# A hybrid decoder layer on one core: a rotary group, three weight splits, two modulation turns and a weave of products change their places

## The chip, the core and the metric

The kernel runs on one core of one Trainium2 chip. The metric is the device time of one launch in microseconds. The kernel before takes 1086.85 us as the median of three runs (1086.14 to 1087.83).

A core has TensorE (PE, matmuls; its weight loads are listed as PEld), VectorE (DVE), ScalarE (ACT), GpSimd (POOL) and SyncE (SP, which here only issues DMAs). Each engine works through its own instructions in a fixed order and waits on semaphores for the others.

## The reference

The layer has two sub-layers on 1024 tokens of width 1024, all in float32. Cut to what matters here:

```python
mod = silu(c) @ w_ada + b_ada
sh1, sc1, g1, sh2, sc2, g2 = split(mod, 6)
h = rmsnorm(x, pre_w_mix) * (1 + sc1) + sh1
aq, ak, av, hq, hf, hi, hg = split(h @ w_in)
aq, ak = partial_rope(aq), partial_rope(ak)      # 16 of each head's 64 dims turn
attn = rmsnorm(sliding_window_sink_attention(aq, ak, av, sinks), attn_out_w)
rec = rmsnorm(hgrn2_chunkwise(silu(hq), 1 - f, hi, log(f)), hg_norm_w) * silu(hg)
x = x + g1 * rmsnorm(concat(attn, rec) @ w_out, post_w_mix)
h = rmsnorm(x, pre_w_mlp) * (1 + sc2) + sh2
x = x + g2 * rmsnorm(square(relu(h @ w_up)) @ w_down, post_w_mlp)
```

Attention has 8 query heads of 64 on 2 key/value heads and a window of 128 tokens, so a block of 128 queries looks at its own block of keys and at the one before.

## The kernel before

**Exact products from rounded parts.** TensorE multiplies numbers in a rounded 32-bit format. Each operand is therefore split: ScalarE copies it into a high half (`hi`, with the names ending in `h`), and VectorE subtracts that from the original to get the low half (`lo`, ending in `l`). A product is three matmuls: high with high, high with low, low with high. `load_split` splits a loaded weight.

**First projection (loop at lines 469 to 523, about 22 to 58 us).** For the first half of the tokens, a loop over the eight 128-wide slices `kb` of the model width turns the normalised x (`first_T`), applies scale and shift while it evicts the result from PSUM (`first_evac`, which makes `hhi` and `hlo`), and multiplies with six weight units: 0 to 3 are queries, 4 is keys, 5 is values (`first_mm`). The scale `a1` and shift `sh1` (with its negative `ns1`) of slices 4, 5 and of 6, 7 come from the conditioning vector: `mod_sum` adds up eight blocks of w_ada on VectorE into `macc`, and `mod_turn` turns the sum on TensorE into `pmt`, reduces it on VectorE and computes `a1`, `sh1` and `ns1`. `mod_turn` is called in the steps kb = 3 and kb = 5, between the units 0 to 3 and the units 4 and 5. In this stage the order on all compute engines is pinned to the order in the program (`pin`).

**The second half of the tokens and attention (lines 700 to 901, about 58 to 188 us; the generator is `attention`, from line 621).** Keys and values of the second half are projected at once; its four query units come later (`q_later`), as pieces of one matmul each in a list, `feed_q`. `feed(us)` takes pieces from that list until the given time is used up at 0.227 us a piece; so it fills TensorE while the softmax of the attention blocks runs on other engines. `weave` mixes the pieces of two units: cuts [6, 9, 12, ...] give six pieces of the one, six of the other, then three of each in turn. Each unit has 24 pieces and needs one of two PSUM banks (`mm_ps`) from its first piece until ScalarE has evicted it behind its last. Behind the queries, `values` puts the value products of the recurrent heads into the same list. Their weights `whv0` to `whv7` are split by `split_hv`.

Attention runs over eight blocks of 128 tokens, as generators that stop between stages, which `step(tb)` moves on:

- stages 1 and 2: scores `sc` on TensorE, mask copy into `comb` on VectorE; maximum `mx`, `nm`, `sd`; eight exponentials with their sums on ScalarE; `den`, `rd` and the scaling of `comb`, half on VectorE and half on GpSimd
- stage 3: `comb` is turned into `pT`; VectorE cuts it into `pc` (own block) and `pp` (block before); `spread` multiplies the block before by its norm (`rb`)
- stage 4: `oT`, the output; its square `sqa`, `aT`, and the sum of squares `sqr`
- stages 5 and 6: `sqr` is turned into `ssp` and summed to `ssc`; GpSimd computes the root; `dg` and the product `rb` spread it

**Rotary.** A query or key tile has its turning rows gathered by DMA (`gather`, three DMAs a tile), multiplied by tables and added (`rotate`, three VectorE instructions on 96 or 64 rows), and scattered back by DMA (`scatter`). For the second half of the tokens there are two groups: group 0 holds two query units and the keys, group 1 the other two query units. Both are done by `rope_late` and `scatter_late`, at the end of block 0's round.

**What sets the order.** In this stage the order of TensorE is pinned, that of SyncE until the end of block 0's round. VectorE, ScalarE and GpSimd are not pinned; the compiler orders them. A few steps are told to follow a marked instruction: `rope_late`, `split_hv` and `mod_sums` take a mark ("sqr", "rb", "omlb", "dg"), which is the latest instruction recorded under that name, and all VectorE instructions of that call are placed somewhere behind it. `mod_sums(n)` moves the sums for the gate g1 and for the second sub-layer on by n blocks of w_ada; the list holds 27 such moves, nine to a sum, and what is left of them runs behind the last block.

After attention come the recurrent heads (products `phf`, `phq`, `phg`), the output projection and the MLP.

Of the kernel before, what the change touches and what calls it, by code (L numbers as in the profile page):

```python
# [13 lines left out]
ALU = mybir.AluOpType  # L14
AX = mybir.AxisListType

P = 128
D = 1024
KB = D // P
# [28 lines left out]
def hybrid_layer(ctx: ExitStack, tc: tile.TileContext, I, out, dbg=None):  # L48
    nc = tc.nc
    ACT, DVE, POOL, PE, SP = (Queue(tc, e) for e in (nc.scalar, nc.vector, nc.gpsimd, nc.tensor, nc.sync))  # L50
# [281 lines left out]
    def mod_turn(q, mk):  # L332
        pst = mk(f"pmt{q[0]}")
        for j in range(4):
            PE.transpose(pst[:, j * P:(j + 1) * P], macc1[q][:, j * P:(j + 1) * P], ident)
        red = small.tile([P, 4], F32, tag="mred", name=f"mred1_{q[0]}")
        DVE.tensor_reduce(red, pst.rearrange("p (j k) -> p j k", j=4), AX.X, ALU.add)
        c = slice(2 * q[0], 2 * q[0] + 2)
        s2 = small.tile([P, 2], F32, tag="m1s", name=f"m1s{q[0]}")
        DVE.tensor_tensor(s2, red[:, 2:4], bT[:, 8 + c.start:8 + c.stop], ALU.add)  # L340
        DVE.tensor_tensor(sh1[:, c], red[:, 0:2], bT[:, c], ALU.add)
        DVE.scalar_tensor_tensor(a1[:, c], s2, 1.0, prew1s[:, c], ALU.add, ALU.mult)
        DVE.tensor_scalar(ns1[:, c], sh1[:, c], -1.0, None, ALU.mult)
# [67 lines left out]
    def first_mm(kb, us, part, ts=slice(0, 512)):  # L411
        bh, bl = (h[:, ts] for h in hh[kb][0])
        for u in us:
            pst, (ah, al) = pu[u][:, ts], unit(u, kb)
            if part == 0:
                PE.matmul(pst, lhsT=ah, rhs=bh, start=(kb == 0 and ts.start == 0), stop=False)
                PE.matmul(pst, lhsT=al, rhs=bh, start=False, stop=False)
            else:
                PE.matmul(pst, lhsT=ah, rhs=bl, start=False, stop=(kb == KB - 1))
# [49 lines left out]
    for kb in range(1, KB):  # L469
        q = nextq.get(kb)  # L470
        if kb == 3:
            mod_sum((2, 0), (7,))
        if kb == 7:
            rbx = tp_ps("rbx")
            PE.matmul(rbx, lhsT=ones, rhs=dgx.rearrange("p a t -> p (a t)"), start=True, stop=True)
        first_evac(0, kb, xT0[kb])
        if kb + 1 < KB:
            first_wq(kb + 1)
        else:
            for j in range(3):  # L480
                DVE.tensor_tensor(xT1[j], xT1[j], rbx, ALU.mult)
            first_evac(1, 0, xT1[0])
            first_evac(1, 1, xT1[1])
        if kb == 3:
            norm_scale(0, 1, ACT)
            pin(True, SP)
            for hf in range(2):
                for tb in range(4, TB):
                    load_x(tb, (hf,))
            pin(False, SP)  # L490
        first_mm(kb, range(4), 0)
        if q:
            mod_mm(q)
            mod_copy(q)
        if kb in (3, 5):
            mod_turn((kb // 2 + 1, 0), tp_ps if kb == 3 else a_ps)
        first_mm(kb, (4, 5), 0)
        if kb + 1 < KB:
            first_wql(kb + 1)
        if q:  # L500
            mod_fold(q)
        if kb in (1, 3, 5):
            first_kv((kb + 1) // 2, DVE)
        if kb < 5:
            mod_sum(*{1: ((2, 0), (0, 4, 1)), 2: ((2, 0), (5, 2, 6, 3)),
                      3: ((3, 0), (0, 4, 1)), 4: ((3, 0), (5, 2, 6, 3, 7))}[kb])
        if kb + 1 < KB:
            xT0.append(first_T(0, kb + 1, a_ps if kb in (2, 3, 6) else tp_ps))
        for tb, hf in {4: ((4, 0), (5, 0)), 5: ((6, 0), (7, 0), (4, 1), (5, 1)), 6: ((6, 1), (7, 1))}.get(kb, ()):
            norm_sq(tb, (hf,))  # L510
        if kb in (5, 6):
            for j in range(4 * kb - 20, 4 * kb - 16):
                xT1.append(load_raw(hT_ if j < 6 else m_, f"xT1_{j}", I["xT1"][j]))
        if kb == 6:
            hgw = cload("hgw", [P, 1], pool=tiny1)
            lbt = cload("lbt", [P, 2, 4], pool=tiny1)
            cosT, sinT = ([load_raw(hv_, f"rope{i}_{th}", I["rope"][i, th]) for th in range(2)] for i in range(2))
        if kb == 6:
            norm_rstd(1, 0, 4)
            dgx = t_("dgx", (P, 4, P))  # L520
            DVE.tensor_tensor(dgx, ident.unsqueeze(1).broadcast_to([P, 4, P]),
                              rx[1].unsqueeze(2).broadcast_to([P, 4, P]), ALU.mult)
        first_mm(kb, range(6), 1)
# [17 lines left out]
    marks = {}  # L541

    def feed(us):
        while us > 0 and feed_q:
            fn, w = feed_q.pop(0)
            fn()
            us -= w
# [60 lines left out]
    fle = cload("fle", [P, P], pool=XA)  # L608
# [12 lines left out]
    def attention(tb):  # L621
# [43 lines left out]
        pc = w_(f"pc{tb}", (P, 2, 4, P))  # L665
        pp = w_(f"pp{tb}", (P, 2, 4, P)) if tb else None
        for mp in range(2):
            pT = tp_ps(f"pT{tb}_{mp}")
            for j in range(4):
                PE.transpose(pT[:, j * P:(j + 1) * P], c[:, 4 * mp + j, :], ident)  # L670
            pT3 = pT.rearrange("p (h q) -> p h q", h=4)
            DVE.tensor_tensor(pc[:, mp], pT3, fle.unsqueeze(1).broadcast_to([P, 4, P]), ALU.mult)
            if tb:
                marks["pp"] = DVE.tensor_tensor(pp[:, mp], pT3, pc[:, mp], ALU.subtract).ins
        spread(tb - 1)
        if 3 <= tb <= 5:
            mod_sums(1, "rb")
        yield
        o_ps = tp_ps(f"oT{tb}")
# [13 lines left out]
        sqr = small.tile([P, P], F32, tag="sqr", bufs=1, name=f"sqr{tb}")  # L693
# [10 lines left out]
        rb = pa.tile([P, 512], F32, tag="aps", name=f"rb{tb}")  # L704
# [17 lines left out]
    for kb in range(KB):  # L722
# [4 lines left out]
        if kb < 6:  # L727
            u = (0, 1, 4, 2, 3, 5)[kb]
            t = evac(0, u, pu[u])
# [44 lines left out]
    def rope_late(mark, i):  # L774
        old, DVE.last = DVE.last, marks[mark]
        rotate(r1[2 * i], r1[2 * i + 1], 64 if i else 96, 1)
        DVE.last = old

    def scatter_late(i):
        for j, t in enumerate(qs[1][2:] if i else qs[1][:2] + [ks[1]]):  # L780
            scatter(t, r1[2 * i], j)

    def q_later(u):
        pst = bank(f"pq1_{u}")

        def done():
            gather(evac(1, u, pst()), *r1[2 * (u // 2):2 * (u // 2) + 2], u % 2)

        queue3(pst, [unit(u, kb) for kb in range(KB)], hhalf(1), 0.227, done)
# [11 lines left out]
    def weave(calls, cuts):  # L801
        a = len(feed_q)
        lists = []
        for call in calls:
            call()
            lists.append(feed_q[a:])
            del feed_q[a:]
        for lo, hi in zip([0] + cuts, cuts + [3 * KB]):
            for fns in lists:
                feed_q.extend(fns[lo:hi])  # L810
# [13 lines left out]
        mods += [modcols(3, half, m_, sh2), modcols(4, half, m_, sc2)]  # L824
    for u in range(2):
        q_later(u)
    weave([lambda: q_later(2), lambda: q_later(3)], [6, 9, 12, 15, 18, 21])

    def step(tb):
        if tb < TB:  # L830
            next(att[tb], None)
# [10 lines left out]
    def split_hv(ks, mark):  # L842
        old, DVE.last = DVE.last, marks[mark]
        for kb in ks:
            if kb < 3:
                wv = w_(f"whv{kb}", (P, 2, 512), F32R)
                parts = {"h": wv[:, 0], "l": wv[:, 1]}
                whv.append(load_split(lambda name, dt: parts[name[-1]], f"whv{kb}", None, raw=hvr[kb]))
            else:
                whv.append(load_split(g_, f"whv{kb}", None, raw=hvr[kb]))  # L850
            if kb < 3:
                load_hv(kb + 5)
        DVE.last = old
# [11 lines left out]
    step(1)  # L865
    feed(2.0)
    step(0)
    feed(2.6)
    for t in range(TB):
        step(t)  # L870
        if t == 0:
            split_hv(range(3, 5), "sqr")
            values_all()
        if t == 1:
            split_hv(range(5, 7), "sqr")
        if t == 1:
            mod_sums(1)
        if 1 < t < 6:
            mod_sums(1, "sqr")
        feed(3.3 if t == 0 else 2.2 if t < 6 else 2.8 if t < 7 else 99)  # L880
        step(t + 2)
        if t == TB - 1:
            pin(False, PE)
        step(t)
        step(t + 2)
        feed(1.0 if t < 6 else 1.8)
        if t > 5:
            mod_sums(1, "dg")
        step(t)
        if t == TB - 1:  # L890
            spread(t)
        step(t + 1)
        if t == 0:
            for i in range(2):
                rope_late("rb", i)
                scatter_late(i)
            pin(False, SP)
        if t == 1:
            split_hv(range(7, KB), "rb")
        feed(4.2 if t == 0 else 2.6 if t < 7 else 99)  # L900
    mod_sums(len(sums), "rb")
    gactx.close()
    Z = x1ctx.enter_context(tc.tile_pool(name="poolZ", bufs=1))
# [886 lines left out]
    for step, (_, t, k) in enumerate(order):  # L1790
# [13 lines left out]
        if k >= 3 and t < 3:  # L1804
            tb = t + 4 * th
# [150 lines left out]
```

## Time and profile before

| | |
|---|---|
| median of three runs | 1086.85 us |
| the profiled execution | 1085.65 us |
| its span | 1083.9 us |
| mean granted TensorE clock | 0.996 of full speed |
| VectorE busy | 803.5 us |
| ScalarE busy | 584.9 us |
| GpSimd busy | 357.3 us |

The page gives busy times over the span of one profiled execution, and the timeline lists instructions by their start (us from the start of the span), duration, engine, operation and tiles; in square brackets stands how long the engine was idle before and what ended that. Nearly all instructions have one line, that of the helper that issues them (line 39), so they are told apart by their tiles. Matmuls overlap: one of 512 columns lasts 0.39 us and the next starts 0.22 to 0.23 us behind it. A list of waits gives total microseconds, number and the longest. A table of stretches gives each engine's busy time in the stretch, the granted TensorE clock as a share of full speed, the share of the DMA engines and GB/s.

### The profile page before, as it was taken

How to read it: one execution, taken by the hardware profiler on the slowest of the kernel's cores; microseconds unless marked ns; L12 is line 12 of the kernel's file. 1: busy time of each engine (PE TensorE's matmuls, PEld its weight loads, DVE VectorE, ACT ScalarE, POOL GpSimd, SP SyncE). 2: the span in 40 equal slices, each digit the busy share in tenths (PEclk: the TensorE clock that was granted, in tenths of full speed). 3: DMA queues.
4: the chain of work that ended last, by engine and by line, in shares of the span. 5: the costliest groups of instructions: out<-in, count | busy, mean ns of one | idle time of the engine just before them, and what ended most of it. 6: DMA issues, size and time to landing. Idle time of an engine off the chain costs nothing.

```text
span 1083.9 us, 15842 instructions
## 1 busy us (share of the span) xinstructions
PE 1065.2 (98%) x5339; PEld 865.4 (80%) x5339; DVE 803.5 (74%) x1317; ACT 584.9 (54%) x1205; POOL 357.3 (33%) x449
## 2 busy tenths in 40 slices
PE   8999999999999999999999999999999999999996
PEld 6787666888888888888888888888888888888885
DVE  4876787888766664558877767677777886899786
ACT  4555354446456655576655555555665544455434
POOL 1221111233325653423434344444333434300014
PEclk9999999999999999999999999999999999999998
DMA  9930301644211252323676777767998888997537
GB/s 355 367 117 28 120 1 34 202 146 140 75 59 56 90 177 95 128 89 129 210 257 231 248 244 232 270 222 250 298 378 308 276 291 279 330 307 250 174 96 138
DMA packets 104865, 208.60 MB, mean 192 GB/s; under 512 B 13840, under 2 KB 14352, under 8 KB 104784
## 3 DMA queue, kind: packets, MB, share of 16 engines
q1 hardware_dynamic: 89296, 160.03, 43.0%
q0 software_dynamic: 15200, 47.20, 14.4%
q8 instruction: 42, 0.69, 0.3%
q10 hardware_dynamic: 288, 0.36, 0.1%
q14 instruction: 39, 0.32, 0.1%
HBM read 150.52 MB, written 55.05 MB: 190 GB/s over the span
## 4 chain that ended last, share of the span: by engine, by line
PE 88%; DVE 5%; DMA 4%; ACT 1%; SPq 1%; issue 1%; POOL 0%; DVEq 0%; ACTq 0%; POOLq 0%
PE pda L39 16%; PE pua L39 14%; PE pdc L39 8%; PE po L39 8%; PE puc L39 7%; PE pu L39 4%; PE phg L39 4%; PE phq L39 4%; PE pdb L39 4%; PE phf L39 4%; PE pub L39 4%; PE pv L39 3%; DMA wa<-wada 2%; PE pq L39 2%; PE o L39 1%; PE oT L39 1%
## 5 line engine op out<-in xcount | busy, mean ns | idle before, releaser
L39 POOL TENSOR_TENSOR b<-b,b 128x512 f32<-128x512 f32 x64 | 88.6, 1384 | 214.5 <-DMA b<-w_dn 214.1
L39 ACT ACTIVATE dw<-dwr 128x512 fp32r<-128x512 f32 x72 | 45.4, 630 | 51.4 <-DMA dwr<-td 29.9
L39 ACT ACTIVATE s<-s 128x512 f32<-128x512 f32 x84 | 53.0, 631 | 33.4 <-DVE s L39 32.0
L39 DVE TENSOR_TENSOR acc<-pda,acc 128x512 f32<-128x512 f32 x68 | 46.7, 687 | 18.3 <-PE pda L39 17.7
L39 DVE TENSOR_TENSOR dw<-dwr,dw 128x512 fp32r<-128x512 f32 x72 | 54.5, 758 | 6.9 <-ACT dw L39 6.9
L39 POOL TENSOR_TENSOR rrf<-ssf,mhalf 128x1 f32<-128x1 f32 x7 | 7.7, 1105 | 106.2 <-DVE ssf L39 106.2
L39 POOL DMA_DIRECT2D td<-b x64 | 36.3, 566 | 19.0 <-POOL b L39 19.0
L39 DVE TENSOR_TENSOR wt<-s,wt 128x512 fp32r<-128x512 f32 x42 | 37.1, 883 | 2.4 <-ACT wt L39 2.1
L39 ACT ACTIVATE s<-pua 128x512 f32<-128x512 f32 x28 | 16.7, 597 | 37.3 <-PE pua L39 34.6
L39 ACT ACT_TABLE_LOAD x28 | 35.9, 1283 | 1.7 <-PEq L1949 1.2
L39 POOL DMA_DIRECT2D b<-w_dn x64 | 34.4, 540 | 2.7 <-issue 2.7
L39 DVE SCALAR_TENSOR_TENSOR macc<-wada,cs,macc 128x512 f32<-128x512 f32 x42 | 33.2, 790 | 2.4 <-DMA wada<-wada 1.7
L39 ACT ACTIVATE comb<-comb,nm 128x128 f32<-128x128 f32 x64 | 24.8, 389 | 18.0 <-DVE nm L39 14.0
L39 DVE TENSOR_TENSOR wt<-a,wt 128x512 fp32r<-128x512 f32 x42 | 33.8, 805 | 0.9 <-ACT wt L39 0.9
L39 POOL TENSOR_TENSOR comb<-comb,rd 128x512 f32<-128x512 f32 x8 | 11.8, 1469 | 66.6 <-DVE rd L39 31.2
L39 PE MATMUL pua<-bt_0h,wt 128*128 128x512 f32 x84 | 32.7, 389 | 0.0
L39 PE MATMUL pua<-bt_1h,wt 128*128 128x512 f32 x84 | 32.7, 389 | 0.0
L39 PE MATMUL pua<-bt_2h,wt 128*128 128x512 f32 x84 | 32.7, 389 | 0.0
L39 PE MATMUL pua<-bt_3h,wt 128*128 128x512 f32 x84 | 32.7, 389 | 0.0
L39 ACT ACTIVATE wt<-s 128x512 fp32r<-128x512 f32 x42 | 26.3, 627 | 10.2 <-DVE s L39 10.0
L39 DVE TENSOR_TENSOR acc<-pdc,acc 128x512 f32<-128x512 f32 x36 | 24.7, 685 | 6.9 <-PE pdc L39 6.5
L39 DVE TENSOR_TENSOR s<-puc,s 128x512 f32<-128x512 f32 x14 | 9.7, 691 | 26.9 <-issue 25.5
(794 smaller groups left out, 3698.2 us busy)
## 6 DMA issues: line engine op xcount, KB each, us to landing
dur<-ud SPq DMA_DIRECT2D x112, 256.0 KB, 4.3
wada<-wada SPq DMA_DIRECT2D x64, 256.0 KB, 3.5
b<-w_dn POOLq DMA_DIRECT2D x64, 256.0 KB, 5.0
td<-b POOLq DMA_DIRECT2D x64, 256.0 KB, 3.4
dwr<-td SPq DMA_DIRECT2D x64, 256.0 KB, 4.0
a<-w_u SPq DMA_DIRECT2D x56, 256.0 KB, 4.5
dwr<-w_dn SPq DMA_DIRECT2D x48, 256.0 KB, 4.6
ud<-s SPq DMA_DIRECT2D x42, 256.0 KB, 3.4
```

Source lines behind the costliest of these rows:

```text
L39: ins = op(*args, **kw)
```

## The change

- In the first projection, kb = 3 now multiplies unit 4, then turns the modulation, then multiplies unit 5; kb = 5 multiplies units 4 and 5 and then turns.
- Query units 2 and 3 are woven 15 pieces and 15, then three of each in turn, in place of six and six.
- Rotary group 0 of the second half follows a new mark, block 0's last `pc`, and its scatters are issued there; group 1 stays at the end of block 0's round.
- Value weights 5, 6 and 7 are split behind block 1's `sqr`; before, 5 and 6 were, and 7 behind the multiply by `rb` at the end of block 1's round.
- In block 0's round the second feed grows from 1.0 to 1.5 us and the third shrinks from 4.2 to 3.8.
- One more move of the modulation sums runs in attention, at block 2.

```diff
-        if kb in (3, 5):
-            mod_turn((kb // 2 + 1, 0), tp_ps if kb == 3 else a_ps)
-        first_mm(kb, (4, 5), 0)
+        if kb == 3:
+            first_mm(kb, (4,), 0)
+            mod_turn((2, 0), tp_ps)
+            first_mm(kb, (5,), 0)
+        else:
+            first_mm(kb, (4, 5), 0)
+        if kb == 5:
+            mod_turn((3, 0), a_ps)
...
-            DVE.tensor_tensor(pc[:, mp], pT3, fle.unsqueeze(1).broadcast_to([P, 4, P]), ALU.mult)
+            marks["pc"] = DVE.tensor_tensor(pc[:, mp], pT3, fle.unsqueeze(1).broadcast_to([P, 4, P]), ALU.mult).ins
...
-        if 3 <= tb <= 5:
+        if 2 <= tb <= 5:
             mod_sums(1, "rb")
...
-    weave([lambda: q_later(2), lambda: q_later(3)], [6, 9, 12, 15, 18, 21])
+    weave([lambda: q_later(2), lambda: q_later(3)], [15, 18, 21])
...
     step(0)
+    rope_late("pc", 0)
+    scatter_late(0)
     feed(2.6)
     for t in range(TB):
         step(t)
...
         if t == 1:
-            split_hv(range(5, 7), "sqr")
+            split_hv(range(5, KB), "sqr")
...
-        feed(1.0 if t < 6 else 1.8)
+        feed(1.5 if t == 0 else 1.0 if t < 6 else 1.8)
...
         if t == 0:
-            for i in range(2):
-                rope_late("rb", i)
-                scatter_late(i)
+            rope_late("rb", 1)
+            scatter_late(1)
             pin(False, SP)
-        if t == 1:
-            split_hv(range(7, KB), "rb")
-        feed(4.2 if t == 0 else 2.6 if t < 7 else 99)
+        feed(3.8 if t == 0 else 2.6 if t < 7 else 99)
```

## The prediction

> **What bounds the kernel now.** I read the page first, then the waits of TensorE over the whole program, then the timeline around the longest two, then the granted clock in short stretches.
>
> ```profile
> span 1083.9 us, 15842 instructions
> PE 1065.2 (98%) x5339; PEld 865.4 (80%) x5339; DVE 803.5 (74%) x1317; ACT 584.9 (54%) x1205; POOL 357.3 (33%) x449
> ```
>
> TensorE is busy for 98% of the span, so what can be won without removing matmuls is in its gaps and in stretches at a lower clock. The list of its waits (total us, times, longest) is short:
>
> ```profile
> PE pv L39 <- DVE whv7l L39: 2.3, 1, 2.3
> PE pq L39 <- ACT qT L39: 2.3, 1, 2.3
> PE pmt L39 <- DVE macc L39: 0.8, 1, 0.8
> PE rb L39 <- DVE dg L39: 0.5, 1, 0.5
> PE oT L39 <- DVE pp L39: 0.4, 1, 0.4
> ```
>
> The first three and the last lie beside code that the diff touches. The first gap, in order of time:
>
> ```profile
> 83.25 0.39 PE L39 MATMUL pq<-hlo,wq1h 128*128 128x512 f32 x1
> 83.47 0.39 PE L39 MATMUL pq<-hhi,wq1l 128*128 128x512 f32 x1
> 85.54 0.57 ACT L39 ACTIVATE qT<-pq 128x512 f32<-128x512 f32 x1
> 86.17 0.50 PE L39 MATMUL pq<-hhi,wq0h 128*128 128x512 f32 x1 [2.31 <-ACT qT L39]
> 90.53 0.39 PE L39 MATMUL pq<-hhi,wq2h 128*128 128x512 f32 x1
> ```
>
> Late query products are fed in pieces; a stream of them starts one every 0.22 to 0.23 us (83.25, 83.47). Counting feeds (9, 14, 14, 18, 9, 12 pieces), the row at 86.17 is piece 55: the first of the fourth query unit, woven in after six pieces of the third. It needs the PSUM bank of the second unit, whose eviction sits on ScalarE behind the exponentials of block 0 and ends at 86.11. The row at 90.53 is piece 64.
>
> The second gap, and the same place one block later:
>
> ```profile
> 119.80 0.39 PE L39 MATMUL pv<-whv7h,hhi 128*128 128x512 f32 x1
> 121.77 0.69 DVE L39 TENSOR_TENSOR whv7l<-whv7r,whv7h 128x512 fp32r<-128x512 f32 x1
> 122.52 0.79 PE L39 MATMUL pv<-whv7l,hhi 128*128 128x512 f32 x1 [2.33 <-DVE whv7l L39]
> 126.87 0.50 PE L39 MATMUL pv<-whv7l,hhi 128*128 128x512 f32 x1
> 136.24 0.39 PE L39 MATMUL pv<-whv7l,hhi 128*128 128x512 f32 x1
> 139.00 0.50 PE L39 MATMUL pv<-whv,hhi 128*128 128x512 f32 x1
> ```
>
> A value product waits for the low half of the last value weight, which VectorE splits only behind block 1's multiply by rb. Behind the gap the work is slow too. In the stretches (busy us of PE, PEld, DVE, ACT, POOL; then the clock granted):
>
> ```profile
> 83.00:87.00 4.00, 1.70 (x11) 0.96 (x11) 1.06 (x3) 3.12 (x15) 0.75 (x1) 1.00 0.00 1
> 122.00:126.00 4.00, 3.48 (x9) 1.52 (x11) 1.52 (x4) 1.91 (x9) 1.45 (x1) 0.57 0.51 177
> 126.00:130.00 4.00, 4.00 (x26) 2.49 (x24) 2.06 (x3) 1.20 (x2) 0.00 (x0) 1.00 0.41 151
> 105.00:125.00 20.00, 17.38 (x96) 11.55 (x96) 18.22 (x38) 10.13 (x42) 3.72 (x4) 0.94 0.40 121
> ```
>
> Around the first gap the clock stays at 1.00; from the end of the second gap it is 0.57 over four microseconds, then 1.00 again. VectorE is busy 18.2 of 20 us around there: it is the engine that could be late next.
>
> **The change part by part.** The profiled execution took 1085.65 us with a span of 1083.9; the median of the three runs shown is 1086.85, that is 1.2 us above the profiled one. I make the sum against the profiled time and add the 1.2 at the end.
>
> *Weave of the third and fourth query unit (15, 18, 21).* The order changes, the 48 pieces don't. Piece 55 becomes one of the third unit, whose bank is free, and would start at 83.47 + 0.23 = 83.70 where it starts at 86.17: 2.5 us won. The fourth unit's first piece is now number 64, at 90.53 - 2.5 = 88.0, and its bank is free at 86.11: that wait is gone, with 1.9 us to spare. Gain 2.5 us (bounds 0, if the wait only moves, and 2.5).
>
> *First late rotary group behind block 0's pc.* It issues three VectorE instructions of 96 rows and three scatter transfers on SyncE's in-order queue.
>
> ```profile
> 86.14 1.77 SPq L39 DMA_DIRECT2D r<-qT  x3
> DMA to landing us min/median/max: 2.7/3.1/3.5
> 91.90 1.29 DVE L39 TENSOR_TENSOR pc<-pT,c_fle 128x512 f32<-128x512 f32 x2 [0.29 <-PE pT L39]
> 94.91 0.17 DVE L39 TENSOR_TENSOR den<-sm,es 128x8 f32<-128x8 f32 x1 [1.72 <-ACT comb L39]
> 107.22 1.88 DVE L39 TENSOR_TENSOR r<-r,rope 96x512 f32<-96x512 f32 x3
> ```
>
> Three such operations take 1.88 us (the row at 107.22). Behind pc VectorE idles 1.72 us until block 1's exponentials are summed, so the group fits into a hole and at most 0.2 us of it shows. Its gathers are issued from 86.14 to 87.91 (first row), which no part of the change moves, since the eviction that they follow ends at 86.11; the last is issued at about 87.3 and landed by 90.8 at the latest of the second row. pc ends at 93.19 now; the chain in front of it (copies of the scores, maximum) can start 1.4 to 1.7 us earlier, so it will end at about 91.5: 0.7 us behind the landing. In SyncE's queue the three scatters stand ahead of the gathers of units three and four, which follow evictions that start at 102.31 now: no cost. Only the scores of block 4 use the scattered rows, three blocks later. Cost 0 (bounds 0 and 0.6: if the three run behind block 1's softmax sums, block 0's aT and sqr are that much late).
>
> *Feeds of block 0 (1.5 and 3.8 in place of 1.0 and 4.2): 7 and 17 pieces for 5 and 19.* The count stays; two value pieces now follow the last query piece at once, and need the third unit's bank.
>
> ```profile
> 102.31 1.30 ACT L39 ACTIVATE qT<-pq 128x512 f32<-128x512 f32 x2
> 102.57 0.40 PE L39 MATMUL pq<-hhi,wq7l 128*128 128x512 f32 x1
> ```
>
> The first of these evictions ends at about 102.9, where the value piece would be due at 102.57 + 0.23 = 102.80; with the row-to-row delay of 0.06 seen at 86.11 to 86.17 that is a new wait of 0.2 us (bounds 0 and 0.4).
>
> *Three weight splits behind block 1's sqr.* The product that stalled is due at 119.80 + 0.23 = 120.03 and ran at 122.52: 2.49 us. From that product to the first one behind oT it took 126.87 - 122.52 = 4.35 us; the same sequence one block later takes 139.00 - 136.24 = 2.76 us: 1.59 us lost at the low clock. Together 4.1 us (bounds 2.5, if the low clock has another cause, and 4.1). What is late next is block 2's pp, at the end of a full VectorE queue:
>
> ```profile
> 108.33 1.09 PE L39 MATMUL oT<-pp,v 128*64 128x512 f32 x4
> 110.98 1.52 DVE L39 TENSOR_TENSOR r<-r,r 64x512 f32<-64x512 f32 x1
> 112.43 0.67 DVE L39 TENSOR_TENSOR aT<-oT,c_attw 128x512 f32<-128x512 f32 x1
> 113.03 1.02 DVE L39 TENSOR_REDUCE sqr<-sqa 128x128 f32<-128x512 f32 x1
> 114.58 0.67 DVE L39 TENSOR_TENSOR whv6l<-whv6r,whv6h 128x512 fp32r<-128x512 f32 x1
> 119.98 1.28 DVE L39 TENSOR_TENSOR pp<-pT,pc 128x512 f32<-128x512 f32 x2
> ```
>
> From aT to the end of pp VectorE works nearly without a hole, 121.26 - 112.43 = 8.8 us; a third split adds 0.7 (the row of whv6l), so 9.5. aT starts 4.1 us behind oT of block 1 (112.43 - 108.33), because both rotary groups stand in front of it. Without the first group's 1.9 us that is 2.2 us, or up to 3.1 if the second group's add again takes 1.52 us where three operations of the first take 1.88; so pp ends 11.7 to 12.6 us behind that oT. TensorE without its stall wants pp at about 120.8 (120.03 and three pieces of 0.23), 12.5 us behind it. So the wait is near zero; the third split also pushes block 1's dg, which TensorE's rb wants, by up to 0.7. I take 0.3 us of new waits (bounds 0 and 0.8).
>
> *One modulation sum earlier (block 2 joins 3 to 5).* The sum at block 2 stands where the last split stood (0.48 for 0.69 us, no change); the eighth sum and the subtraction behind it leave the place in front of block 7's pp:
>
> ```profile
> 181.63 0.69 DVE L39 TENSOR_TENSOR mlob_g<-macc,mhib_g 128x512 fp32r<-128x512 f32 x1
> ```
>
> That takes 0.7 us and more off the queue that pp ends, and oT's 0.4 us of waiting (the last wait above) goes. Their new place, behind sqr of block 5, costs VectorE the same 0.7 us, which can push block 5's dg; the nearest row for that is rb's one wait on dg, 0.5 us. Gain 0.4 us (bounds -0.1, the two set against each other, and 0.4).
>
> *Modulation turns behind their products.*
>
> ```profile
> 43.98 0.40 PE L39 MATMUL pq<-hhi,wq5l 128*128 128x512 f32 x1
> 45.14 0.63 PE L39 MATMUL pmt<-c_tab,macc 128*128 128x128 f32 x4 [0.76 <-DVE macc L39]
> 46.80 0.16 DVE L39 TENSOR_SCALAR ns<-sh 128x2 f32<-128x2 f32 x1
> ```
>
> For kb = 5 the turn is 0.93 us late (45.14 - 43.98 - 0.23), and four products of 0.23 now fill that. But the scale and shift (ns, ended 46.96) follow the turn as before, and the next hi half needs them: it can start at 47.0 instead of 47.17 and its products follow 0.8 us later. So most of the 0.9 comes back as a wait there. For kb = 3 the turn's own wait is about 0.3 us, and the delayed turn costs VectorE, which is full, 0.15. Both together: gain 0.3 us (bounds 0 and 0.9).
>
> Sum: 2.5 + 0 - 0.2 + 4.1 - 0.3 + 0.4 + 0.3 = 6.8 us. 1085.65 - 6.8 = 1078.85 for an execution like the profiled one, 1080.0 against the median. Behind 200 us TensorE shows no wait on transfers that an earlier start would bring out, so I carry the whole sum to the end.
>
> The Trainium skill, page "TensorE: Matmul & The Clock Gate", section "Why this matters for your kernels", tells to keep TensorE idle for no more than about 3 us between bursts, since a window of 3.4 us without work halves the clock. This trace is harsher: 2.33 us were followed by the low clock, while 2.31 us were not. By the Trainium skill's rule the low clock would not belong to the gap, and the sum would be 5.2.
>
> **The rivals.**
>
> *The low clock comes back elsewhere.* Against the forecast speaks that one gap of 2.3 us lowered the clock and its twin didn't; so the gap alone doesn't decide, and the fall may hang on something that stays. Then 1.6 us are not won: 1081.6. For the forecast speaks that the low rows begin with the end of the gap. Chance 0.10. The Trainium skill's rule above points the same way as this rival.
>
> *VectorE becomes the bound in block 1.* The 18.2 of 20 us speak for it. If the second group's gathers, or ScalarE's copies, make aT 2 us later than worked out, oT of block 2 waits 2 us, and the clock may fall once more: 3.6 us back, 1083.6. Against: about 1.9 us of work leaves that stretch. Chance 0.11.
>
> *The split doesn't move.* VectorE's order is not pinned here; a mark only says what an instruction follows, and the last split could still be issued behind the multiply by rb. Then 4.1 us less: 1084.1. Against: the other two splits with that mark follow sqr at once (rows from 113.03). Chance 0.06.
>
> *Slower: the moved group blocks VectorE.* In its in-order queue the group stands ahead of block 1's sums and block 0's aT and sqr, and waits for transfers. TensorE turns that sqr in ssp:
>
> ```profile
> 100.19 0.33 PE L39 MATMUL ssp<-c_tab,sqr 128*128 128x128 f32 x1
> ```
>
> It would want it at 100.2 - 2.5 = 97.7. With 1.9 us for the group and about 2.7 for aT, sqr and the sums in front of them (1.7 us by the rows of aT and sqr, 1 us estimated for the rest), landings up to 93.1 cost nothing, each microsecond beyond costs one, and a wait over 2.3 us adds 1.6 for the clock. It ends slower once the landing is later than 93.1 + 5.2 = 98.3, that is 11 us behind the issue at 87.3; landing at 100 gives 1080.0 + 6.9 + 1.6 = 1088.5. Measured landings are 2.7 to 3.5 us. Chance 0.03.
>
> **How the numbers follow.** The forecast has 0.66; smaller mixtures (a bank wait that stays in part, new short waits) the remaining 0.04. Its bounds alone: the moved group at 0.6, the waits at 0.4 and 0.8, the sum at -0.1 and the turns at 0 add 0.6 + 0.2 + 0.5 + 0.5 + 0.3 = 2.1 and give 1082.1; all at their best take off 0.2 + 0.3 + 0.6 = 1.1 and give 1078.9. The runs shown lie up to 1.0 us from their median. The range goes from 1078.0 up to 1083.6, which takes in the first two rivals. A measurement of this kernel can tell about 0.2%, 2.2 us, from no change; nearly all cases but the last lie beyond that on the fast side: faster 0.93, same 0.04, slower 0.03.
>
> **What would show it.** Right: no wait of pv on whv7l and none of pq on qT, a clock of 1.00 from 110 to 130 us, whv7l directly behind whv6l on VectorE, the 96-row rotation between pc of block 0 and den of block 1, and the first head product (phf) 6 to 7 us earlier than now. Wrong: a wait of oT on pp or rb on dg over 1 us in block 1 or 2, a low clock anywhere before 190, a wait of VectorE on the gathers, or a head product that starts early while the span does not shrink.

## The result, and the profile after

The changed kernel takes 1080.49 us (median of six executions, 1080.08 to 1080.77) where the kernel before takes 1086.75 us on the same chip (six executions, 1086.06 to 1087.83). The ratio is 0.9942, with a 95% interval of 0.9929 to 0.9954; by the medians that is 6.3 us less. The forecast was 1080.0. One of its terms had the wrong sign, though, and one hung on where a gap happens to fall in an execution; the two partly cancel, so a part of the nearness is luck.

The profiled execution took 1080.08 us. The top of the page of the changed kernel, as span and busy times:

```profile
span 1078.3 us, 15841 instructions
PE 1063.7 (99%) x5339; PEld 864.4 (80%) x5339; DVE 795.4 (74%) x1317; ACT 584.3 (54%) x1205; POOL 355.8 (33%) x449
```

The number of TensorE instructions is the same, and the span is 5.6 us shorter. The list of TensorE's waits in the changed kernel (total us, times, longest):

```profile
PE rb L39 <- DVE dg L39: 1.5, 2, 0.9
...
PE oT L39 <- ACT comb L39: 0.5, 1, 0.5
PE oT L39 <- DVE pp L39: 0.5, 1, 0.5
```

The two waits of 2.3 us are gone. New are a longer wait of rb and a wait of oT that has comb on ScalarE at its end.

The first gap closed as worked out. The timeline of TensorE in the changed kernel at that place:

```profile
82.52 0.39 PE L39 MATMUL pq<-hhi,wq1l 128*128 128x512 f32 x1
82.75 0.39 PE L39 MATMUL pq<-hhi,wq2h 128*128 128x512 f32 x1
...
87.00 0.39 PE L39 MATMUL pq<-hhi,wq0h 128*128 128x512 f32 x1
```

The piece behind wq1l comes 0.23 us later, and the fourth unit's first piece, at 87.00, has no bracket: it waits for nothing. The second place, first on VectorE and then on TensorE, in the changed kernel:

```profile
88.84 1.28 DVE L39 TENSOR_TENSOR pc<-pT,c_fle 128x512 f32<-128x512 f32 x2
90.04 1.28 DVE L39 TENSOR_TENSOR r<-r,rope 96x512 f32<-96x512 f32 x2
91.35 0.69 DVE L39 TENSOR_TENSOR r<-r,r 96x512 f32<-96x512 f32 x1
92.21 0.17 DVE L39 TENSOR_TENSOR den<-sm,es 128x8 f32<-128x8 f32 x1 [0.17 <-ACT comb L39]
...
111.25 0.68 DVE L39 TENSOR_TENSOR whv7l<-whv7r,whv7h 128x512 fp32r<-128x512 f32 x1
...
116.65 1.28 DVE L39 TENSOR_TENSOR pp<-pT,pc 128x512 f32<-128x512 f32 x2
```

```profile
116.71 0.39 PE L39 MATMUL pv<-whv7l,hhi 128*128 128x512 f32 x1
118.08 1.09 PE L39 MATMUL oT<-pp,v 128*64 128x512 f32 x4 [0.52 <-DVE pp L39]
```

The rotary group fills the hole between block 0's pc and block 1's den; den still waits 0.17 us for ScalarE, so nothing was pushed. whv7l ends at 111.93, 4.8 us before TensorE uses it. What is late next is block 2's pp, by 0.52 us, the place that the prediction named. The granted clock in stretches of the changed kernel (the clock stands third from the end):

```profile
82.00:86.00 4.00, 4.00 (x42) 3.27 (x41) 1.22 (x4) 4.00 (x19) 0.71 (x1) 1.00 0.02 4
...
114.00:118.00 4.00, 3.56 (x20) 2.69 (x18) 3.97 (x10) 1.30 (x8) 0.00 (x0) 1.00 0.97 336
118.00:122.00 4.00, 3.92 (x16) 2.12 (x17) 2.83 (x7) 3.43 (x14) 1.40 (x1) 1.00 0.48 182
```

It is 1.00 throughout. To see where the time went, I set the starts of the same TensorE instructions in the two traces against each other:

| TensorE instruction | before | after | shift | what changed on the way |
|---|---|---|---|---|
| xT, second group | 16.75 | 16.09 | -0.66 | no part of the change: the first tokens landed sooner |
| late queries (wq1h) | 69.90 | 68.95 | -0.95 | modulation turns: 0.3 won |
| oT of block 0 | 94.46 | 90.93 | -3.53 | weave: 2.58 won |
| oT of block 1 | 108.33 | 105.07 | -3.26 | wait for a bank: 0.27 lost |
| oT of block 3 | 137.12 | 130.32 | -6.80 | splits and clock: 3.54 won |
| oT of block 5 | 161.36 | 154.59 | -6.77 | nothing |
| rb of block 5 | 169.43 | 163.69 | -5.74 | 1.03 lost |
| oT of block 6 | 173.48 | 168.34 | -5.14 | 0.60 lost |
| oT of block 7 | 184.86 | 179.26 | -5.60 | 0.46 regained |

From there on the shift stays between 5.4 and 5.6 us. So 1.6 us were lost around block 5, where only the modulation sum differs. VectorE there, first before and then in the changed kernel, from block 5's sum of squares to its dg:

```profile
165.21 1.05 DVE L39 TENSOR_REDUCE sqr<-sqa 128x128 f32<-128x512 f32 x1
166.18 0.74 DVE L39 SCALAR_TENSOR_TENSOR macc<-wada,cs,macc 128x512 f32<-128x512 f32 x1
167.18 0.29 DVE L39 TENSOR_REDUCE ssc<-ssp 128x1 f32<-128x128 f32 x1 [0.26 <-PE ssp L39]
...
168.42 0.29 DVE L39 TENSOR_SCALAR dg<-c_tab,r_att 128x128 f32<-128x128 f32 x1 [0.26 <-POOL r_att L39]
```

```profile
158.44 1.05 DVE L39 TENSOR_REDUCE sqr<-sqa 128x128 f32<-128x512 f32 x1
159.41 0.74 DVE L39 SCALAR_TENSOR_TENSOR macc<-wada,cs,macc 128x512 f32<-128x512 f32 x1
160.85 0.69 DVE L39 TENSOR_TENSOR mlob_g<-macc,mhib_g 128x512 fp32r<-128x512 f32 x1 [0.69 <-ACT mhib_g L39]
161.46 0.77 DVE L39 COPY_PREDICATED comb<-c_mle,sc 128x256 f32<-128x256 int32 x2
162.12 0.28 DVE L39 TENSOR_REDUCE ssc<-ssp 128x1 f32<-128x128 f32 x1
163.35 0.29 DVE L39 TENSOR_SCALAR dg<-c_tab,r_att 128x128 f32<-128x128 f32 x1 [0.95 <-POOL r_att L39]
```

Behind the eighth block of a modulation sum comes more than an addition: ScalarE copies the finished sum into its high half (mhib_g), and VectorE subtracts that from the sum (mlob_g). In VectorE's in-order queue the subtraction waits 0.69 us for the copy, takes 0.6, and a mask copy of 0.66 now stands ahead of ssc too. From sqr to ssc it takes 162.12 - 158.44 = 3.68 us where it took 167.18 - 165.21 = 1.97: 1.71 us, and dg is late by the same (4.91 for 3.21).

### The profile page after: what moved, and what is told of

It reads as the page before. It is cut to its first block, busy times and chain, and to the rows that moved or that the text cites. A ratio compares the mean times of both kernels' runs of the same rounds, so it can differ in the third digit from the quotient of the medians.

```text
span 1078.3 us, 15841 instructions
## 1 busy us (share of the span) xinstructions
PE 1063.7 (99%) x5339; PEld 864.4 (80%) x5339; DVE 795.4 (74%) x1317; ACT 584.3 (54%) x1205; POOL 355.8 (33%) x449
## 4 chain that ended last, share of the span: by engine, by line
PE 92%; DVE 4%; ACT 1%; DMA 1%; POOL 0%; issue 0%; DVEq 0%; ACTq 0%
PE pda L39 16%; PE pua L39 14%; PE pdc L39 8%; PE po L39 8%; PE puc L39 7%; PE pq L39 4%; PE pu L39 4%; PE phg L39 4%; PE phq L39 4%; PE pdb L39 4%; PE phf L39 4%; PE pub L39 4%; PE pv L39 3%; PE o L39 1%; PE sc L39 1%; PE oT L39 1%
## 5 line engine op out<-in xcount | busy, mean ns | idle before, releaser
L39 DVE TENSOR_TENSOR dw<-dwr,dw 128x512 fp32r<-128x512 f32 x72 | 57.4, 797 | 10.2 <-ACT dw L39 10.2
L39 DVE TENSOR_TENSOR wt<-a,wt 128x512 fp32r<-128x512 f32 x42 | 29.5, 702 | 0.9 <-ACT wt L39 0.9
L39 PE MATMUL pda<-dw,du_7h 128*128 128x512 f32 x96 | 29.5, 389 | 0.0
```

Of the source, the lines that this page charges most:

```text
L39: ins = op(*args, **kw)
```

## The experiments

Each kernel was run beside the kernel before on the same chip. Where a shift is given, it compares the starts of the same TensorE instructions with the trace of the changed kernel.

**One part put back: the weave.**

```diff
-    weave([lambda: q_later(2), lambda: q_later(3)], [15, 18, 21])
+    weave([lambda: q_later(2), lambda: q_later(3)], [6, 9, 12, 15, 18, 21])
```

> The changed kernel with the weave of query units 2 and 3 back at six and six pieces. Theory: the wait of the fourth unit's first piece on the second unit's eviction comes back at 2.3 us, and little else: 1083.0. If the granted clock falls behind this gap, as it did in the kernel before behind the other gap of 2.3 us, 1.6 us more: 1084.6. Rival: the wait only moved in the changed kernel, and the time stays at 1080.5.

Measured: 1084.85 us (11 executions, 1082.83 to 1086.56), ratio to before 0.998 (0.9971 to 0.9989). The wait, and the clock around it, in this kernel's trace:

```profile
PE pq L39 <- ACT qT L39: 2.3, 1, 2.3
```

```profile
82.00:86.00 4.00, 3.29 (x15) 2.39 (x13) 1.66 (x5) 2.22 (x12) 0.00 (x0) 1.00 0.41 124
86.00:90.00 4.00, 2.40 (x17) 1.97 (x19) 1.06 (x3) 1.54 (x7) 1.45 (x1) 0.69 0.11 29
90.00:94.00 4.00, 4.00 (x32) 3.45 (x31) 2.69 (x5) 1.83 (x5) 0.00 (x0) 0.89 0.03 8
```

The same gap that kept the clock in the profile of before loses it here. The shift goes from +2.39 to +6.47, 4.1 us: 2.5 for the gap and 1.6 for the clock. The executions fall into two groups: three of 1082.83 to 1083.02 us at a mean clock of 0.998, and eight of 1084.30 to 1086.56 at 0.994 to 0.997. So the low clock isn't bound to the second gap, and comes in some executions only. The two slowest of the eight have means of 0.994 and 0.995, which is too low for one such stretch. The profiled execution is one of them: it starts 2.4 us behind the changed kernel, with a gap of 1.85 us in which TensorE waits for its first tokens, and behind that gap the clock is low too (0.50 from 8.99 to 12.41 us).

**One part put back: the last split.**

```diff
-            split_hv(range(5, KB), "sqr")
+            split_hv(range(5, 7), "sqr")
...
+        if t == 1:
+            split_hv(range(7, KB), "rb")
```

> The changed kernel with the last value weight's split back behind block 1's multiply by rb. The product that needs it is due at 116.7 us and the split would end at about 118.4: a gap of about 1.8 us, which takes in the 0.5 us that oT waits on pp now. Theory (the gap lowers the clock): low clock behind it, 1.3 + 1.6 = 2.9 us slower than the changed kernel, 1083.4. Rival (the low clock of the kernel before has another cause, or needs a longer gap): 1.3 us slower, 1081.8.

Measured: 1083.48 us (7 executions, 1081.83 to 1084.75), ratio 0.9974 (0.9963 to 0.9985). The wait and the clock in its trace:

```profile
PE pv L39 <- DVE whv7l L39: 2.4, 1, 2.4
```

```profile
116.00:120.00 4.00, 1.56 (x7) 0.69 (x7) 3.44 (x9) 3.64 (x18) 0.13 (x1) 1.00 0.21 78
120.00:124.00 4.00, 4.00 (x18) 2.10 (x14) 2.01 (x4) 1.42 (x3) 1.32 (x1) 1.00 0.82 257
```

Here it is the second gap that keeps the clock. That execution was one of the fastest (1081.83) and its shift is 1.6 us, less than the 2.4 of the wait, since 0.5 us of waiting on pp lies in its shadow and block 1's rb, which no longer waits behind the third split, starts 0.2 us sooner. Three executions lie at 1081.83 to 1082.36, the other four at 1083.48 to 1084.75, with lower means (0.994 to 0.997).

**One part put back: both rotary groups behind rb.**

```diff
-    rope_late("pc", 0)
-    scatter_late(0)
...
-            rope_late("rb", 1)
-            scatter_late(1)
+            for i in range(2):
+                rope_late("rb", i)
+                scatter_late(i)
```

> The changed kernel with both late rotary groups behind block 0's multiply by rb, as before. Theory: VectorE has 1.9 us more ahead of block 1's aT, so ssp, rb and oT of block 2 are late; the wait of oT on pp of 0.5 us and that of rb grow to about 2 us together: 1082.0, with the low clock 1083.6. Rival: the group costs nothing there either, since it fills the same kind of hole behind rb: 1080.5.

Measured: 1081.46 us (1081.32 to 1081.54), ratio 0.9956 (0.9944 to 0.9969). Two rows of TensorE's timeline in this kernel:

```profile
114.76 0.49 PE L39 MATMUL rb<-dg,ones 128*128 128x128 f32 x2 [1.07 <-DVE dg L39]
119.41 1.09 PE L39 MATMUL oT<-pp,v 128*64 128x512 f32 x4 [0.54 <-DVE pp L39]
```

With the first group back in block 1's stretch, dg is 1.1 us late. So the move of the group by itself costs nothing, and it makes room worth 1.1 us for the third split; the weave and this split are not the whole change. All five executions stay at a mean clock of 0.997 to 0.998: a gap of 1.07 us lowered it in none.

**One part alone: the three splits behind block 1's sqr, in the kernel before.**

```diff
         if t == 1:
-            split_hv(range(5, 7), "sqr")
+            split_hv(range(5, KB), "sqr")
...
-        if t == 1:
-            split_hv(range(7, KB), "rb")
```

> The kernel before with the three value weights split behind block 1's sqr, and nothing else changed. Theory: the gap of 2.3 us and the low clock go together (4.1 us); both rotary groups still stand ahead of aT, so oT of block 2 waits about 1 us on pp: 3.1 us faster than before, 1083.7. Rival (the low clock is not the gap's doing): 1.5 us faster than before, 1085.2.

Measured: 1084.71 us (11 executions, 1082.75 to 1085.42), ratio 0.9983 (0.9974 to 0.9992). Waits and one stretch of its trace:

```profile
PE rb L39 <- DVE dg L39: 1.5, 2, 1.1
PE oT L39 <- DVE pp L39: 1.0, 2, 0.5
```

```profile
86.00:90.00 4.00, 4.00 (x34) 3.75 (x34) 1.10 (x3) 0.82 (x3) 1.22 (x1) 0.57 0.15 37
```

The split alone brings 1.9 us by the medians, not 4.1: block 1's rb now waits 1.1 us and block 2's oT 0.5 us (its full waits also hold older ones of 0.4 to 0.5), and the first gap, which stays, lowers the clock in this execution. The executions fall into groups here too: four of 1082.75 to 1083.41 us and seven of 1084.63 to 1085.42.

**Two small parts put back: the feeds, and the modulation turns.**

```diff
-        feed(1.5 if t == 0 else 1.0 if t < 6 else 1.8)
+        feed(1.0 if t < 6 else 1.8)
...
-        feed(3.8 if t == 0 else 2.6 if t < 7 else 99)
+        feed(4.2 if t == 0 else 2.6 if t < 7 else 99)
```

> The changed kernel with block 0's feeds back at 1.0 and 4.2 us. Theory: the two value pieces no longer follow the last query piece, the bank wait of about 0.2 us goes and nothing takes its place, since dg is ready 0.9 us ahead of rb: 1080.2. Rival: the longer feed covers a wait of rb on dg or of pT; then such a wait shows behind the last query piece and the time is 1080.7 or more. The times can hardly tell these apart, the starts of sc, rb and oT in the profile can.

```diff
-        if kb == 3:
-            first_mm(kb, (4,), 0)
-            mod_turn((2, 0), tp_ps)
-            first_mm(kb, (5,), 0)
-        else:
-            first_mm(kb, (4, 5), 0)
-        if kb == 5:
-            mod_turn((3, 0), a_ps)
+        if kb in (3, 5):
+            mod_turn((kb // 2 + 1, 0), tp_ps if kb == 3 else a_ps)
+        first_mm(kb, (4, 5), 0)
```

> The changed kernel with the two modulation turns back ahead of their products. Theory: TensorE loses 0.3 us between the steps kb = 3 and kb = 7, with the wait of pmt on macc back at 0.76 us: 1080.8. Rival: the 0.95 us by which the changed kernel leads at the end of that loop all come from the turns, and the time is 1081.4; the lead of 0.65 us at the very start, ahead of the loop, would then be gone as well.

Measured: 1081.24 us (1079.98 to 1081.92; ratio 0.995, 0.9938 to 0.9963) for the feeds and 1081.23 (1080.76 to 1082.87; ratio 0.9954, 0.9941 to 0.9968) for the turns; their spreads are too wide for a few tenths, so the traces must tell. Both profiled executions lose another 1.3 us between 940 and 955 us, in the MLP, where products wait for VectorE's acc; no edit touches that place, so the shifts are read ahead of it. With the old feeds the wait for a bank is gone and 0.27 us are won at oT of block 1, and lost again at block 1's rb, which waits for dg (the kernel's rb waits are 1.8 us in three places). From there on its shift is the one that it had at the start: the feeds are worth nothing. With the old turns the wait of pmt on macc is back (1.0 us in two places) and the products of the first projection lose 0.36 us to the changed kernel's.

**The modulation sum: three ways to move it.** First, block 2's extra sum left for the end:

```diff
-        if 2 <= tb <= 5:
+        if 3 <= tb <= 5:
             mod_sums(1, "rb")
```

> The changed kernel without the additional modulation sum at block 2, so that the eighth sum and its two copies leave the place behind block 5's sqr. Theory: TensorE loses 1.65 us of its lead at blocks 5 and 6 because VectorE there waits 0.69 us for ScalarE's copy of the sum and runs the sum and the subtraction ahead of ssc, so that dg is late (wait of rb 0.86, of oT 0.54). Without it these waits go and oT of block 7 waits 0.4 us on pp again: 1079.3, that is 1.2 us faster than the changed kernel. Rival: TensorE, 6.8 us ahead, has only caught up with a chain that was always that long; then the waits stay and the time is 1080.5.

Second, the eighth sum behind block 5's rb:

```diff
-        if 1 < t < 6:
+        if 1 < t < 5:
             mod_sums(1, "sqr")
...
+        if t == 5:
+            mod_sums(1, "rb")
```

> The changed kernel with block 2's sum kept, and the eighth sum (block 5's round) placed behind block 5's multiply by rb in place of behind its sqr. Theory: the waits of rb and oT in blocks 5 and 6 go, and oT of block 7 stays without its wait on pp: 1078.9, 1.6 us faster than the changed kernel. If ScalarE's copy of the sum lands among block 7's exponentials, up to 0.6 us of that comes back, at pT of block 7. Rival (the chain itself is that long): 1080.5.

Third, the eighth sum at block 6's dg, where it was before the change, together with the ninth move:

```diff
-        if 1 < t < 6:
+        if 1 < t < 5:
             mod_sums(1, "sqr")
...
         if t > 5:
-            mod_sums(1, "dg")
+            mod_sums(2 if t == 6 else 1, "dg")
```

> The changed kernel with block 2's modulation sum kept, none behind block 5's sqr, and two at block 6's dg, so that the eighth sum and its subtraction stand where they stood before the change while the stretch behind block 7 gets no longer. Theory (the eighth sum ahead of block 5's dg is what costs): the waits of rb and oT in blocks 5 and 6 (1.65 us) go, the wait of oT(7) on pp (0.4 to 0.5) comes back, nothing else moves: 1.2 us under the changed kernel, 1079.3. Rival (VectorE is full from block 2 on, and the sum costs the same wherever it stands): another wait of about 1 us on dg, ssp or pp takes their place, 1080.3 to 1080.7.

| | median (range) | ratio to before | shift from oT of block 5 to oT of block 6 | then |
|---|---|---|---|---|
| first | 1079.36 (1078.72 to 1081.54) | 0.9938 (0.9925 to 0.995) | 1.63 won | 0.5 lost at oT(7), 1.1 at phg |
| second | 1079.76 (1079.59 to 1080.74) | 0.994 (0.9927 to 0.9952) | 1.63 won | 1.2 lost at ssp of block 6 |
| third | 1079.03 (1078.94 to 1079.90) | 0.993 (0.9916 to 0.9944) | 1.63 won | 0.45 lost at oT(7), 0.2 won behind |

All three win the same 1.63 us at the same place, so the eighth sum ahead of block 5's dg is what cost it. What they do with it differs. (The profiled executions of the first and the third are the slowest of their five: against the changed kernel's trace the first is 1.8 us late from the start, and the third loses 1.2 us in the MLP at about 943 us.) The first has one more sum behind block 7, and the recurrent heads then wait 0.82 us for ScalarE (that the longer rest of the sums is the cause is argued, not shown); the second puts the subtraction in front of block 6's aT and sqr:

```profile
212.39 0.50 PE L39 MATMUL phg<-hhi,whg0h 128*128 128x512 f32 x1 [0.82 <-ACT f L39]
```

```profile
169.58 1.53 DVE L39 TENSOR_TENSOR mlob_g<-macc,mhib_g 128x512 fp32r<-128x512 f32 x1
171.03 0.68 DVE L39 TENSOR_TENSOR aT<-oT,c_attw 128x512 f32<-128x512 f32 x1
```

```profile
172.78 0.30 PE L39 MATMUL ssp<-c_tab,sqr 128*128 128x128 f32 x1 [1.08 <-DVE sqr L39]
```

The first fence is the first kernel's TensorE, the other two are VectorE and TensorE of the second. The third kernel has VectorE free where block 5 needs it:

```profile
158.38 1.05 DVE L39 TENSOR_REDUCE sqr<-sqa 128x128 f32<-128x512 f32 x1
160.36 0.29 DVE L39 TENSOR_REDUCE ssc<-ssp 128x1 f32<-128x128 f32 x1 [0.92 <-PE ssp L39]
...
161.59 0.29 DVE L39 TENSOR_SCALAR dg<-c_tab,r_att 128x128 f32<-128x128 f32 x1 [0.26 <-POOL r_att L39]
```

It stands 1.4 us under the changed kernel run beside it, 1.2 expected. That comparison run, with no edit:

> The changed kernel once more, as the comparison for the three others of this group: 1080.5 us, no wait of pv on whv7l, and the waits of rb (0.9) and oT (0.5) in blocks 5 and 6 again.

It took 1080.44 us (1080.38 to 1081.03), ratio 0.9944 (0.9931 to 0.9956).

**A version that beats both.** Value weight 5 is split one block earlier, alone and on top of the third kernel above:

```diff
-            split_hv(range(3, 5), "sqr")
+            split_hv(range(3, 6), "sqr")
...
-            split_hv(range(5, KB), "sqr")
+            split_hv(range(6, KB), "sqr")
```

> The changed kernel with value weight 5 split behind block 0's sqr alone. Theory: the 0.5 us wait of oT(2) on pp goes, 1080.0. Rival (nothing won, or a new wait in block 0): 1080.5 to 1081.0.

> As the kernel with the eighth sum at block 6's dg, and value weight 5 is split behind block 0's sqr in place of block 1's, into a hole of 0.9 us that VectorE has there ahead of ssc. Theory (block 1's stretch still ends on VectorE's queue, as the 0.5 us wait of oT(2) on pp shows): that wait goes and nothing is late in block 0, 1.6 to 1.7 us under the changed kernel, 1078.8. Rival (the third split only delays block 0's dg or block 1's pp instead): a wait of 0.3 to 0.7 us in block 0 or 1, 1079.3 to 1079.7.

Measured: alone 1080.15 us (1079.69 to 1080.48), ratio 0.994 (0.9928 to 0.9953); with the eighth sum moved 1078.34 us (1078.14 to 1078.69), ratio 0.9924 (0.991 to 0.9937). VectorE of the latter, in block 0:

```profile
96.50 0.68 DVE L39 TENSOR_TENSOR whv5l<-whv5r,whv5h 128x512 fp32r<-128x512 f32 x1
97.46 0.29 DVE L39 TENSOR_REDUCE ssc<-ssp 128x1 f32<-128x128 f32 x1 [0.28 <-PE ssp L39]
```

The split goes into the hole, and ssc still waits 0.28 us for TensorE. Between oT of block 1 and scores of block 4 the shift falls by 0.61 us (0.59 in the kernel with the split alone). By the medians the split alone is 0.3 us, within the spread of its executions; both together are 2.1 us, and 1.9 in the trace (the shift goes from +0.43 to -1.49). Against 1086.55 us of the kernel before, run beside it, that version is 8.2 us faster.

## Why the prediction was right, and the step of it that failed

*The weave*: 2.5 predicted, 2.58 measured. Right, with the mechanism as told: nothing in the bank's way any more.

*The rotary group*: at no cost, as predicted. The room that it makes was counted in the prediction's chain from aT to pp, and the experiment that puts it back shows its size, 1.1 us.

*The feeds*: 0.2 of waiting predicted, 0.27 measured, but it is worth nothing in the end, since rb waits for dg instead without it.

*The splits*: 4.1 less 0.3 of new waits predicted, 3.54 measured with 0.52 of waiting on pp. Right within 0.3 us.

*The modulation turns*: 0.3 predicted; 0.30 in the trace of the change, 0.36 where it is put back.

*The modulation sum* is the step that failed: "Gain 0.4 us (bounds -0.1, the two set against each other, and 0.4)". The 0.4 at block 7's pp did come (0.46), but 1.6 us were lost in front of it: the net is a loss of 1.2 us (1.03 + 0.60 - 0.46), outside the bounds. The prediction priced the subtraction by its own 0.69 us, and took an old wait of 0.5 us as the price of late dg. It left out that the subtraction waits 0.69 us for a copy on ScalarE while everything behind it on VectorE stands still, and that the mask copy gets ahead of ssc in the time. In its old place, block 6's dg, another step of VectorE lay between the eighth block of the sum and the subtraction (at 181.63 before), and covered the copy, which ScalarE made there from 180.97 to 181.60; VectorE before, at that place:

```profile
180.85 0.69 DVE L39 TENSOR_TENSOR aT<-aT,rb 128x512 f32<-128x512 f32 x1
```

*The low clock*. The prediction read one profile as a rule: one gap lowers the clock, its twin doesn't, so the 1.6 us belong to the second. The runs show each gap with and without the low clock. The traces show what decides: in each of the fourteen, the times between changes of the clock are whole multiples of 3.413 us, so the clock changes only at the edges of a fixed raster, and it is low behind a stretch of the raster in which TensorE idled long enough. Three gaps, in stretches of that raster; the first four rows are the kernel before, the last two the kernel with the last split behind rb:

```profile
81.59:85.00 3.41, 2.27 (x11) 1.54 (x9) 0.67 (x4) 2.65 (x14) 0.00 (x0) 1.00 0.27 91
85.00:88.41 3.41, 2.24 (x33) 2.00 (x33) 1.26 (x4) 1.73 (x7) 1.45 (x1) 1.00 0.12 32
...
119.14:122.55 3.41, 1.08 (x6) 0.57 (x4) 3.32 (x9) 2.52 (x14) 0.00 (x0) 1.00 0.33 117
122.55:125.96 3.41, 3.41 (x9) 1.45 (x11) 1.06 (x3) 1.36 (x5) 1.45 (x1) 0.50 0.59 205
```

```profile
114.07:117.48 3.41, 2.35 (x12) 1.60 (x10) 3.41 (x9) 1.50 (x8) 0.00 (x0) 1.00 0.77 288
117.48:120.89 3.41, 2.03 (x9) 0.99 (x11) 2.38 (x6) 2.38 (x11) 1.02 (x1) 1.00 0.26 59
```

An edge cuts the first gap of the kernel before in halves of 1.1 and 1.2 us (PE busy 2.27 and 2.24 of 3.41), and the clock stays; the second gap lies whole in one stretch (busy 1.08), and the next is low. With the last split behind rb an edge cuts the same gap, and the clock stays. Where the raster stands against the gap differs from execution to execution, so the outcome does too.

Of 23 executions of the kernel before, run beside the experiments on weave, splits and rotary group, ten took 1085.04 to 1085.75 us at a mean clock of 0.996 to 0.997 and thirteen 1086.49 to 1088.28 at 0.994 to 0.995. A low stretch like that of the profile lowers the mean by 0.0016 (3.44 us at half speed, from the 0.57 of four microseconds, in 1084). So I read the groups as one and two low stretches; only the profiled execution, of the first group, has a trace. None of the 23 is without a low stretch by this reading. That fits the raster: the two gaps start 36.3 us apart, 10.6 of its stretches, so an edge that halves the first gap leaves the second nearly whole (an estimate from the trace of the kernel before). The changed kernel has neither gap, stays at 0.997 to 0.998, and its six executions lie within 0.7 us.

This also corrects how the median was reached. The prediction added 1.2 us, the distance of the profiled execution from the median, as if it stayed. By this reading it was mostly the second low stretch, which the change removes: the changed kernel's median lies 0.4 us above its profiled execution. That made up for part of what the modulation sum lost, which is why the time came out so near: the forecast got the median right partly by luck. The profiled executions themselves differ by 5.57 us: 0.66 at the start, which no part of the change touches, and 4.9 from the parts (0.3 + 2.58 - 0.27 + 3.54 - 1.63 + 0.46 = 4.98, less about 0.05 behind block 7). Against 6.8 forecast 1.9 are missing, and 1.6 of them are the modulation sum (0.4 won against 1.2 lost).

*The rivals*. VectorE became the bound in block 1, but by 0.5 us and not by 2. The split and the rotary group moved as the code says, and no transfer was waited for. The first rival's price (1.6 us for the clock) was right, and its condition wrong: the low clock didn't come back elsewhere, because TensorE's longest wait left in this stage is 0.9 us. Of the signs that the prediction named, one failed: the first head product (phf) starts 5.6 us earlier (182.42 for 188.00), not 6 to 7, which is the loss of the modulation sum.

What stays open is the last few tenths between the medians (6.3) and the sum of the parts with one and a half low stretches (4.9 + 0.5 x 1.6 = 5.7); the start of the program and the MLP at 940 us vary by that much and more from run to run.

## What to carry to other kernels

When a step moves to another place in an in-order queue, list all that the step issues at that count, on the other engines too: the last of a series of equal moves may end with a copy elsewhere and a wait for it, and that wait holds up whatever stands behind it. Put such a pair where the instruction that TensorE needs next stands ahead of it. And before a stall is priced by one profile, look at the spread of the times: two groups 1.6 us apart mean that part of the price differs from execution to execution.

## What the runs showed of the hardware

A kernel with one gap of 2.3 to 2.4 us on TensorE had a low clock in most executions and none in others (by the groups of times eight of eleven with the old weave, four of seven with the last split behind rb; in two of each group the mean clock is low enough for a second low stretch, and a gap at the start of the program made one of them); a gap of 1.07 us did so in none of five. What counts is how much of the gap lies in one stretch of the 3.413 us raster: in all fourteen traces, from the first rise of the clock on, each stretch in which TensorE idled 1.85 us or more was followed by a low one (1.85, 2.21 with the old weave, 2.29 with the splits alone, 2.32 in the kernel before, more at the programs' ends), and no stretch with 1.61 us or less was. Where the clock fell between gaps, it was for one stretch, 3.41 us at half speed. The Trainium skill, page "TensorE: Matmul & The Clock Gate", section "What's actually happening", has a free-running window of 3.4 us behind the clock. The raster and the length of the low stretches agree with it; but by that section a whole idle window is needed, and here 1.85 us of idling in one were enough.

VectorE's subtraction mlob_g, which reads two tiles, took 1.53 us in place of 0.69 when it started beside GpSimd's scaling of comb. GpSimd in the kernel with the eighth sum behind rb:

```profile
169.10 1.46 POOL L39 TENSOR_TENSOR comb<-comb,rd 128x512 f32<-128x512 f32 x1 [7.62 <-ACT mhib_g L39]
```

It ends at 170.56, and mlob_g, started at 169.58, ends 0.55 us behind that: it did most of its work only when GpSimd was done. The Trainium skill, page "SBUF — State Buffer", section "SBUF: two separate sides", says that the two share a pair of ports that one holds for a whole instruction, and that a VectorE operation with two inputs in SBUF needs it; the trace agrees with 1.53 for 0.69 us. This is a part of what the second of the three moves lost at block 6's ssp.
